# One decoder layer on one core: an expert's two column halves split over the contraction, or two experts side by side

## The chip, the cores and the metric

The kernel runs on 1 core of one Trainium2 chip. The metric is the device time of one execution in microseconds (us). Engines are named as in the profile: PE (TensorE, matrix products; its weight loads are listed as PEld), DVE (VectorE), ACT (ScalarE), POOL (GpSimd) and SP (SyncE, which issues the weight transfers).

## What is computed

One decoder layer over 512 tokens of width 1024: three attention branches, a gated merge with an output projection, a layer norm, then a mixture of 32 experts and a second norm. The change lies in the experts. Cut to that part, the reference is:

```
def hierarchical_moe(x, ...):
    # top-1 group of 4, then top-2 of the 8 experts in it; gate = p(group) * softmax(top-2 logits)
    ...
    def expert_block(args):
        xb, e = args
        h = jax.nn.silu(xb @ w_gate[e]) * (xb @ w_up[e])     # [1024, 512] each
        return h @ w_down[e]                                 # [512, 1024]
    ...
    y_assign = y_pad[dest] * gate_sorted[:, None]
    out = jax.ops.segment_sum(y_assign, tok_sorted, num_segments=N)
```

## The kernel before

**Stages.** Projections and attentions run first, then the output projection with the first norm and the routing, up to about 452 us of the profile. The rest is the experts, then the second norm. Everything the experts read is float32, and all 32 experts' weights are streamed: 32 x 6 pieces of 1 MB.

**Slots.** Each expert gets 64 slots, so a pair of experts (2p, 2p+1) fills 128 partitions. `Pair.select` (L720) makes a 0-1 matrix [token, slot]; `gather` (L729) multiplies it with the residual x1 (for p of 2 and more with `xb`, x1 as three bfloat16 parts made by `split3`, L798) to get the pair's inputs `xg`; `info` (L741) fetches the gates and token numbers `si`; `places` (L756) makes the opposite 0-1 matrix `sT`; `combine` (L779) multiplies `sT` with the pair's outputs `y_h` and `y_l` (high and low part) and DVE adds the result to x1 (L791).

**One expert.** `up` (L945) is one of the two products with a [1024, 512] matrix: 8 matmuls of 512 columns whose stationary operand is the 64 slots of one expert, so each uses 64 of the array's 128 columns. `colmm` (L938) sends the even contraction tiles to partitions 0 to 63 of a PSUM bank and the odd ones to 64 to 127; `fold` (L929) then adds the two halves with one ACT copy (L933) and one DVE add (L935). `hidden` (L953) is silu on ACT and the product with the gate on DVE, `turn` (L957) four transpositions and an ACT copy to `hT`, `down` (L971) the two halves (c = 0, 1) of the third product, each 4 matmuls, a fold, and a split into `y_h` and `y_l`.

**Order of the work.** PE runs the order in which the code is written (`manual_schedule`). The other engines' orders are chosen by a scheduler from the dependencies. `expert(e)` (L988) runs up (gate), the transpositions of the expert before, a part of the pair's gather or combine, up (up), then the third product of the expert before. PSUM has eight banks by tags: `gu` 2, `dn` 2, `cb` 2, `xgp` 1, `ht` 1; a gather uses `xgp`, `turn` and `info` use `ht`, and a combine of a token tile writes two banks, `cb` and `cb`, or `xgp` and `ht`.

**Weights.** A ring of 16 pieces (four pools) and five pieces in tiles that are free for a while (`xb`, `once`) hold the weights; SP issues the transfers in their order of use, each as soon as its ring tile is free. After expert 17 stands a loop over slots beyond an expert's 64 (L1139), which with these inputs runs no iteration. All engines meet at a barrier ahead of it. Ten pieces are requested ahead of the loop, and six ring tiles are given to its body.

**The end.** `last_expert` (L1047) and `last_sums` (L1065) finish the sums; the factors and offsets of the second norm are brought to all partitions by four matmuls with a row of ones (`spread`, L979).

Of the kernel before, what the change touches and what calls it, by code (L numbers as in the profile page):

```python
# [38 lines left out]
AHEAD = (10, 11, 2, 20, 21)  # L39
# [3 lines left out]
MID = 17  # L43
# [8 lines left out]
def layer(ctx, tc, xT, xn, memT, w_qk, w_v, w_mk, w_mv, w_g, w_o, rb, oh, ln, wr, br,  # L52
# [76 lines left out]
    # Projections run as jobs of a queue, each on one loaded weight tile, in pieces that fill  # L129
    # the tensor engine between the steps of the attentions.  # L130
# [39 lines left out]
    def proj_T(rhs_h, rhs_l, n, done):  # L170
        """128 columns of a projection, transposed: [column, token]"""
        def body(w):
            o = bank("pj")
            for k in range(0, KT, 2):
                mm3(o[:, :n], [(w[0][:, j * P:(j + 1) * P], w[1][:, j * P:(j + 1) * P], rhs_h[:, j, :], rhs_l[:, j, :])
                               for j in (k, k + 1)], start=k == 0, stop=k == KT - 2)
                yield 6 * max(n, 256) / 512 * 0.216
            done(o)
        return body

    def put_q(res):
        """per head of the pair: [hi; hi] and [lo; lo] of q / 8"""
# [13 lines left out]
    def put_k(res, n=S, dst=None):  # L196
        """per head of the pair: hi in its own half, lo in the other"""
# [10 lines left out]
    def add_v(name, first, v):  # L208
        """[token, head dims] of a branch's values, two token tiles at a time"""
# [26 lines left out]
    # softmax attention, one pair of heads and one tile of queries at a time  # L236
# [50 lines left out]
    def advance(unit, us):  # L287
        """one more unit of softmax attention enters; those inside go one step further"""
# [11 lines left out]
    # stick-breaking attention: weight = sigmoid(z_s) times the product of 1 - sigmoid(z_j) = sigmoid(-z_j)  # L300
    # over the keys j after s, up to the query
# [19 lines left out]
    # memory keys and values  # L321
# [46 lines left out]
    # 0 for keys before the query, else far below any score  # L368
# [82 lines left out]
    # 128 columns of the model width at a time: gates times branch outputs, then their part of the  # L451
    # output projection, added to the residual
# [75 lines left out]
    def fetch(e, j, c, t=None):  # L528
        """half of one of an expert's three weight matrices"""
# [11 lines left out]
    def prefetch(e, j, cs=(0, 1), ts=(None, None)):  # L541
        for c, t in zip(cs, ts):
            pieces[e, j, c] = fetch(e, j, c, t)
# [8 lines left out]
    for ct in range(6):  # L552
# [7 lines left out]
        if ct in (2, 4):  # L560
            lastw[0] = jobs.last
            prefetch(ct // 2 - 1, 0)
# [19 lines left out]
    def norm(t, sm, gb, sp):  # L582
        """layer norm of x1's tile t, whose sums lie in sm"""
# [25 lines left out]
    prefetch(1, 1, ts=(t[:, 0:HALF], t[:, HALF:2 * HALF]))  # L609
    prefetch(0, 2, ts=(t[:, 2 * HALF:], None))  # L610
    prefetch(1, 2)
    prefetch(2, 0)
    prefetch(2, 1, (0,))
# [31 lines left out]
    def route(t, xts):  # L645
# [8 lines left out]
        # the group with the largest logit, then the two largest experts in it  # L654
# [33 lines left out]
    def settle():  # L688
        """the weights of every token's two experts, and the tables of the slots"""
# [18 lines left out]
    class Pair:  # L708
        """the slots of experts 2p and 2p + 1: their tokens, gates, inputs and outputs"""
# [10 lines left out]
        def select(self, t, d=None):  # L720
            """who sits in the slots, as a 0-1 matrix [token, slot]"""
# [19 lines left out]
        def info(self):  # L741
# [10 lines left out]
            ve.tensor_copy(si[0:64, 3:4], sp[64:128, 1:2])  # L752
            self.gate = (si[0:64, 0:1], si[0:64, 3:4])
# [11 lines left out]
        def room(self, c, dt=F32R):  # L765
            """half the columns of y, as the sum of two parts if in F32R"""
# [31 lines left out]
    def split3(c):  # L798
        """half the columns of x1 as the sum of three bfloat16"""
# [23 lines left out]
    def project(t, cols=(0, 1)):  # L823
        """the rest of the output projection of a token tile, and its norm"""
# [84 lines left out]
        # (base + hi - 1) * 64 + (rank - 64 * hi), or a negative number for ranks below 64  # L909
# [5 lines left out]
    # experts  # L915
# [7 lines left out]
    prefetch(0, 1, ts=(t[:, 0:HALF], t[:, HALF:]))  # L923
    prefetch(2, 1, (1,))
    prefetch(3, 0)
    prefetch(3, 1)
    prefetch(2, 2, (0,))
    after(sc.preload_act_table(AF.Silu), last_act[0])
    def fold(dst, src, q=0):  # L929
        """the two column halves of a product, added, to dst if given"""  # L930
        a, b = H[q], H[1 - q]
# [21 lines left out]
    def hidden(g, u, gate):  # L953
        sc.activation(out=g, in_=g, func=AF.Silu)
        ve.scalar_tensor_tensor(out=u, in0=u, scalar=gate, in1=g, op0=ALU.mult, op1=ALU.mult)

    def turn(u):  # L957
        hp = bank3("ht")
        for k in range(4):
            pe.transpose(hp[:, k * 64:(k + 1) * 64], u[:, k * P:(k + 1) * P], ident[0:64, 0:64])  # L960
        hT = late[0].tile([P, 4, 64], F32, name="hT", tag="hT", bufs=2)
        sc.copy(hT.rearrange("p a b -> p (a b)"), hp[:, 0:256])
        return hT

    def product(e, hT, c):
        w = weights(e, 2, c)
        o = bank3("dn")
        colmm(o, 4, lambda k: hT[:, k, :], lambda k: w[:, k * 512:(k + 1) * 512])
        return o

    def down(e, hT, c):  # L971
        pair, q = pairs[e // 2], e % 2
        if q == 0:
            pair.room(c, F32 if e == NE - 2 and c == 1 else F32R)
        pair.finish(c, q, product(e, hT, c))
# [3 lines left out]
    def spread(t, c):  # L979
        """512 of the second norm's factors and offsets to every partition"""  # L980
        r = slice(c * 512, (c + 1) * 512)
        o = bank3("xgp")
        pe.matmul(o, ones[0], t[0][0:1, r], start=True, stop=True)  # L983
        sc.copy(t[1][:, r], o)

    held, lnb2, ones = [None], [], [None]

    def expert(e):  # L988
        """an expert's first two products; the third of the expert before it, and what its pair waits for"""
# [280 lines left out]
```

## Time and profile before

| what | value |
|---|---|
| time, three runs | 994.44 us median (994.25 to 994.84) |
| the profiled execution: its span, first to last instruction (its only own time on the page) | 995.3 us |
| PE busy / share of the span | 955.3 us / 96% |
| DVE busy | 585.9 us / 59% |
| ACT busy | 379.1 us / 38% |
| POOL busy | 31.4 us / 3% |
| bytes moved, mean rate | 248.64 MB, 250 GB/s |
| PE granted clock, mean | 0.986 |

A busy PE is the share of time in which a matmul record is open; records of neighbouring matmuls overlap, so how long a piece of work takes on PE is read from the start of its first record to the start of what follows. "x16" in a row counts merged records: one float32 matmul is two records.

### The profile page before, as it was taken

The page shows a single profiled execution, that of the slowest core. Times are in us where ns is not written, and L with a number is a line of the kernel's source. Part 1 is how long each engine was busy: PE and PEld are TensorE (multiplying, and loading weights), DVE is VectorE, ACT ScalarE, POOL GpSimd, SP SyncE. Part 2 cuts the span into 40 slices and gives each one's busy share as a digit, 9 for nine tenths or more (in the row PEclk, how much of TensorE's full clock was granted, in tenths as well). Part 3 has the DMA queues.
Part 4 walks back from the last instruction along what each step waited for, and adds up shares of the span by engine and source line. Part 5 has one row for each costly group of instructions (what it writes and reads, how often), then busy time and mean ns, then how long its engine had stood idle before and what let it go on. Part 6 is the DMA issues. An engine that isn't in the chain of part 4 may idle for free. (4 is left out here: it accounts for less than half of the span.)

```text
span 995.3 us, 14993 instructions
## 1 busy us (share of the span) xinstructions
PE 955.3 (96%) x5892; PEld 612.4 (62%) x5892; DVE 585.9 (59%) x1210; ACT 379.1 (38%) x707; POOL 31.4 (3%) x24
## 2 busy tenths in 40 slices
PE   6999999999999999999999999999979999999992
PEld 6888888776888888784644544545525445455331
DVE  5776777556655532787766455554454556544457
ACT  6465565546222223234623333323313333233333
POOL 2000000000000000410000000000000000000003
PEclk9999999999999999999999999999989999999996
DMA  8252332121644332688799999999938999997902
GB/s 298 64 157 72 101 107 76 52 85 44 239 151 157 118 104 87 231 358 351 274 359 376 408 394 393 391 397 403 390 148 312 415 421 420 420 419 301 411 2 85
DMA packets 43938, 248.64 MB, mean 250 GB/s; under 512 B 5682, under 2 KB 6873, under 8 KB 19417
## 3 DMA queue, kind: packets, MB, share of 16 engines
q1 hardware_dynamic: 42194, 246.80, 64.6%
q10 hardware_dynamic: 1672, 0.85, 0.4%
q8 instruction: 48, 0.79, 0.3%
q14 instruction: 24, 0.20, 0.1%
HBM read 245.53 MB, written 2.11 MB: 249 GB/s over the span
## 5 line engine op out<-in xcount | busy, mean ns | idle before, releaser
L940 PE MATMUL gu<-r,xg 128*64 128x512 f32 x992 | 228.8, 603 | 5.3 <-DVE sel L726 5.3
L940 PEld LDWEIGHTS gu<-r,xg 128*64 128x64 f32 x992 | 67.5, 138 | 130.5 <-issue 126.2
L104 DVE TENSOR_TENSOR wl<-wraw,wh 128x1024 fp32r<-128x1024 f32 (+2 forms) x71 | 81.0, 1146 | 85.8 <-ACT wh L103 85.6
L125 PE MATMUL pj<-xh,wh 128*128 128x512 f32 x304 | 120.6, 397 | 0.0
L126 PE MATMUL pj<-xh,wl 128*128 128x512 f32 x304 | 118.6, 390 | 1.1 <-DVE wl L104 1.1
L127 PE MATMUL pj<-xl,wh 128*128 128x512 f32 x304 | 118.7, 391 | 0.0
L940 PE MATMUL dn<-r,hT 128*64 128x512 f32 x504 | 114.8, 596 | 0.0
L933 ACT COPY lo<-gu 64x512 f32<-64x512 f32 x64 | 37.3, 583 | 189.4 <-PE gu L940 185.7
L103 ACT CAST wh<-wraw 128x1024 fp32r<-128x1024 f32 (+2 forms) x71 | 70.3, 990 | 77.5 <-PE z L127 23.5
L738 PEld LDWEIGHTS <-xb 128*128 128x128 bf16 x1344 | 75.1, 98 | 13.1 <-issue 12.2
L738 PE MATMUL xgp<-sel,xb 128*128 128x128 bf16 x1344 | 79.9, 219 | 0.0
L940 PEld LDWEIGHTS dn<-r,hT 128*64 128x64 f32 x504 | 34.4, 137 | 68.5 <-issue 66.3
L935 DVE TENSOR_TENSOR u<-gu,lo 64x512 f32<-64x512 f32 x32 | 21.7, 679 | 86.5 <-ACT lo L933 86.5
L125 PEld LDWEIGHTS pj<-xh,wh 128*128 128x128 f32 x304 | 57.0, 188 | 14.3 <-issue 2.1
L791 DVE TENSOR_TENSOR x<-x,cb 128x512 f32<-128x512 f32 x61 | 40.0, 675 | 43.7 <-PE cb L789 43.7
L126 PEld LDWEIGHTS pj<-xh,wl 128*128 128x128 f32 x304 | 57.1, 188 | 12.8 <-DVE wl L104 1.4
L127 PEld LDWEIGHTS pj<-xl,wh 128*128 128x128 f32 x304 | 57.1, 188 | 12.1
L933 ACT COPY lo<-dn 64x512 f32<-64x512 f32 x64 | 37.0, 577 | 67.8 <-PE dn L940 67.7
L104 DVE TENSOR_TENSOR y_l<-yo,y_h 64x512 fp32r<-64x512 f32 x62 | 42.5, 686 | 31.1 <-ACT y_h L103 29.9
L103 ACT CAST y_h<-yo 64x512 fp32r<-64x512 f32 x62 | 38.2, 617 | 50.5 <-DVE yo L935 50.4
L935 DVE TENSOR_TENSOR g<-gu,lo 64x512 f32<-64x512 f32 x32 | 21.8, 682 | 54.7 <-ACT lo L933 54.7
L935 DVE TENSOR_TENSOR yo<-dn,lo 64x512 f32<-64x512 f32 x62 | 42.7, 689 | 10.6 <-ACT lo L933 6.0
(622 smaller groups left out, 1444.8 us busy)
## 6 DMA issues: line engine op xcount, KB each, us to landing
r<-in_we_dram SPq DMA_DIRECT2D x186, 1024.0 KB, 8.5
wraw<-in_w_g_dram SPq DMA_DIRECT2D x32, 512.0 KB, 3.5
wraw<-in_w_qk_dram SPq DMA_DIRECT2D x14, 512.0 KB, 3.7
wraw<-in_w_v_dram SPq DMA_DIRECT2D x16, 384.0 KB, 3.3
wraw<-in_w_o_dram SPq DMA_DIRECT2D x8, 512.0 KB, 3.6
xb<-in_we_dram SPq DMA_DIRECT2D x3, 1024.0 KB, 7.0
xraw<-in_xT_dram SPq DMA_DIRECT2D x4, 512.0 KB, 6.2
x<-in_xn_dram SPq DMA_DIRECT2D x4, 512.0 KB, 5.8
```

Of the source, the lines that this page charges most:

```text
L103: sc.copy(dst_h, src)
L104: (gp if eng is gp else ve).tensor_tensor(out=dst_l, in0=src, in1=dst_h.bitcast(F32), op=ALU.subtract)
L125: pe.matmul(o, lh, rh, start=start and i == 0, stop=False)
L126: pe.matmul(o, ll, rh, start=False, stop=False)
L127: pe.matmul(o, lh, rl, start=False, stop=stop and i == n - 1)
L738: pe.matmul(o[:, j * P:(j + 1) * P], a, b, start=i == 0, stop=i == len(srcs) - 1)
L791: ve.tensor_tensor(out=x1[:, t, r], in0=x1[:, t, r], in1=o, op=ALU.add)
L933: sc.copy(lo[a], src[b])
L935: ve.tensor_tensor(out=dst[a], in0=src[a], in1=lo[a], op=ALU.add)
L940: pe.matmul(o[H[k % 2]], lhs(k), rhs(k), start=k < 2, stop=k >= n - 2)
```

## The change

Two experts of a pair now run side by side. `up(p, j)` and `down(p, hT, c)` alternate matmuls of expert 2p (to partitions 0 to 63) and of expert 2p+1 (64 to 127), each over its whole contraction, so a bank holds the finished product of both and nothing is folded (the loop over extra slots, which runs no iteration, keeps `colmm` and `fold`). Silu, gating, transposition and the split of the output are done once per pair on 128 partitions. `pair_step(p)` is: up (gate) of the pair; combine of token tiles 0 and 1 of the pair before; up (up); combine of tiles 2 and 3; the first half of the next pair's gather; the transpositions; the second half of the gather and `info`; the third product. The third product is no longer held back into the next expert.

The weights are requested by a list in the new order of use (`todo`, `ahead`), 14 pieces ahead of the loop instead of 10, and the loop's body shares two ring tiles. The factors of the second norm come by two broadcast transfers in place of `spread`. `turn` needs one `hT` of 128 columns instead of two of 64.

```diff
     def weights(e, j, c):
-        return pieces.pop((e, j, c)) if isinstance(e, int) and (e, j, c) in pieces else fetch(e, j, c)
+        if (e, j, c) not in pieces:
+            ahead(1)
+        return pieces.pop((e, j, c))
+
+    def pieces_of(p):
+        return [(e, j, c) for j in range(3) for c in range(2) for e in (2 * p, 2 * p + 1)]
+
+    todo = [x for p in range(16) for x in pieces_of(p)]
+    todo[4:15] = todo[4:6] + todo[8:15] + todo[6:8]
+    taken = [0]
+
+    def ahead(n, ts=()):
+        for i in range(n):
+            e, j, c = todo[taken[0]]
+            taken[0] += 1
+            pieces[e, j, c] = fetch(e, j, c, ts[i] if i < len(ts) else None)
...
-        def finish(self, c, q, o, inplace=False):
+        def finish(self, c, o):
             if self.y_h[c] is None:
-                fold(self.y_l[c], o, q)
+                sc.copy(self.y_l[c], o)
             else:
-                y = fold(None if inplace else ep.tile([P, 512], F32, name="yo", tag="g", bufs=1), o, q)
-                split(self.y_h[c][H[q]], self.y_l[c][H[q]], y[H[q]])
+                split(self.y_h[c], self.y_l[c], o)
...
-    def up(e, q, pair, j, t):
-        w = [weights(e, j, c) for c in range(2)]
+    def up(p, j):
         o = bank3("gu")
-        colmm(o, KT, lambda k: pair.xg[:, k, H[q]], lambda k: w[k // 4][:, k % 4 * 512:k % 4 * 512 + 512])
-        fold(t, o)
-        return t
+        for k in range(KT):
+            for q in range(2):
+                if k % 4 == 0:
+                    w = held[q] = weights(2 * p + q, j, k // 4)
+                pe.matmul(o[H[q]], pairs[p].xg[:, k, H[q]], held[q][:, k % 4 * 512:k % 4 * 512 + 512],
+                          start=k == 0, stop=k == KT - 1)
+        return o
...
+    def hidden(p, g, u):
+        gs = ep.tile([P, 512], F32, name="g", tag="g", bufs=1)
+        hs = ep.tile([P, 512], F32, name="u", tag="u", bufs=1)
+        sc.activation(out=gs, in_=g, func=AF.Silu)
+        ve.scalar_tensor_tensor(out=hs, in0=u, scalar=pairs[p].si[:, 0:1], in1=gs, op0=ALU.mult, op1=ALU.mult)
+        return hs
...
+    def down(p, hT, c):
+        pair = pairs[p]
+        pair.room(c, F32 if p == 15 and c == 1 else F32R)
         o = bank3("dn")
+        w = [weights(2 * p + q, 2, c) for q in range(2)]
+        for k in range(4):
+            for q in range(2):
+                pe.matmul(o[H[q]], hT[:, k, H[q]], w[q][:, k * 512:(k + 1) * 512], start=k == 0, stop=k == 3)
+        pair.finish(c, o)
...
+    def pair_step(p):
+        g = up(p, 0)
+        if p > 0:
             pairs[p - 1].combine((0,))
             pairs[p - 1].combine((1,), banks=("xgp", "ht"))
+        u = up(p, 1)
+        hs = hidden(p, g, u)
+        if p == 0:
             once.close()
             late[0] = ctx.enter_context(pool("late", side="right", waits="tile"))
             split_gates()
+        else:
+            pairs[p - 1].combine((2,))
+            pairs[p - 1].combine((3,), banks=("xgp", "ht"))
+        if p < 15:
+            pairs[p + 1].gather(0)
+        hT = turn(hs)
+        if p < 15:
+            pairs[p + 1].gather(1, "cb" if p == 0 else "xgp")
+            pairs[p + 1].info()
+        for c in range(2):
+            down(p, hT, c)
+        if p == 0:
             xb[0] = xbp.tile([P, 3, TT, D], BF16, name="xb", tag="xb")
             split3(0)
             split3(1)
             for t in range(TT):
                 sc.mul(x1[:, t, :], x1[:, t, :], ALPHA)
+        if p == 1:
             overflow_table()
+        if p != MIDP:
+            pairs[p].places()
+        if p == 15:
+            lnt = ring().rearrange("p (a b) -> p a b", b=D)
+            lnb2.append(lnt)
+            for i in range(2):
+                nc.sync.dma_start(lnt[:, i, :], ln[2 + i:3 + i, :].to_broadcast([P, D]))
...
-        experts(range(MID + 1))
-    for h in AHEAD:
-        prefetch(MID + h // 10, h % 10)
+        steps(range(MIDP + 1))
+    ahead(RA + RB + RC + RD - 2)
...
-        experts(range(MID + 1, NE - 1))
-        last_expert()
+        pairs[MIDP].places()
+        steps(range(MIDP + 1, 16))
```

How the instructions stand, at three places. First PE in the middle of the experts, before: the second half of a combine (L788, L789), then the third product (`dn`), which reads weights and `hT` alone.

```order
L788 MATMUL xgp<-y_h_4998,sT 128x512
L789 MATMUL xgp<-y_l_4999,sT 128x512
L788 MATMUL ht<-y_h_5013,sT 128x512
L789 MATMUL ht<-y_l_5014,sT 128x512
L940 MATMUL dn<-r_5303,hT 64x512 x4
L940 MATMUL dn<-r_5318,hT 64x512 x4
L940 MATMUL gu<-r_5342,xg 64x512 x4
L940 MATMUL gu<-r_5344,xg 64x512 x4
L960 MATMUL ht<-ident,u 128x64 x4
```

The same place of PE in the changed kernel: the same combine (now L796, L797), then at once the gather (L748) into the bank `xgp`.

```order
L796 MATMUL xgp<-y_h_5142,sT 128x512
L797 MATMUL xgp<-y_l_5143,sT 128x512
L796 MATMUL ht<-y_h_5159,sT 128x512
L797 MATMUL ht<-y_l_5160,sT 128x512
L748 LDWEIGHTS xb
L748 MATMUL xgp<-sel,xb 128x128
```

Between a combine that fills `xgp` and a gather that fills it again there stood a third product, an up product and transpositions; now nothing stands there. Second, VectorE around the same place, before: the adds of the combine (L791) with the fold (L935) and the gating (L955) between them.

```order
L791 TENSOR_TENSOR x_2546<-x_2546,cb 128x512
L935 TENSOR_TENSOR u<-gu,lo 64x512
L791 TENSOR_TENSOR x_2546<-x_2546,cb 128x512
L955 SCALAR_TENSOR_TENSOR u<-u,si,g 64x512
L791 TENSOR_TENSOR x_2546<-x_2546,xgp 128x512
L791 TENSOR_TENSOR x_2546<-x_2546,ht 128x512
```

VectorE there in the changed kernel: the gating (L967) of 128 partitions, then the four adds (L799), then `sT` (L770).

```order
L967 SCALAR_TENSOR_TENSOR u<-gu,si,g 128x512
L799 TENSOR_TENSOR x_2546<-x_2546,cb 128x512 x2
L799 TENSOR_TENSOR x_2546<-x_2546,xgp 128x512
L799 TENSOR_TENSOR x_2546<-x_2546,ht 128x512
L770 TENSOR_TENSOR sT<-si,cs 128x512
```

The add that empties `xgp` still stands behind the gating and two adds; one fold has gone. Third, VectorE at the end of the first pair, before: the last of `split3` (L805, L807; `r` is its remainder), the first pair's `sT` (L761), the selection of the third pair (L725, L726) and the next fold.

```order
L807 TENSOR_TENSOR xb<-r_4403,xb 128x512
L807 TENSOR_TENSOR xb<-r_4408,xb 128x512
L761 TENSOR_TENSOR sT<-si,cs 128x512
L725 TENSOR_SCALAR sel<-i128b,d_3752 128x128 x2
L726 SCALAR_TENSOR_TENSOR sel<-i128b,d_3752,sel 128x128 x2
L760 TENSOR_TENSOR si<-si,cs 128x4
L935 TENSOR_TENSOR g<-gu,lo 64x512
```

VectorE there in the changed kernel: the last of `split3` (L813, L815), `sT` (L770), which shares a tile with half of `split3`'s remainders, and at once the adds of the first combine.

```order
L813 TENSOR_TENSOR r_4361<-x_2546,xb 128x512
L815 TENSOR_TENSOR xb<-r_4356,xb 128x512
L770 TENSOR_TENSOR sT<-si,cs 128x512
L815 TENSOR_TENSOR xb<-r_4361,xb 128x512
L799 TENSOR_TENSOR x_2546<-x_2546,cb 128x512 x2
```

In both kernels `split3` can begin when the third product has read the piece that lies in `xb`. Before, the rest of the third products, the second pair's gather, three up products and the third pair's gather then stand on PE ahead of the first combine, which needs `sT`; now half of the third product and one up product of the pair (twice 16 records) stand there.

## Rows read from the trace of the kernel before

**Rows 1.** Windows: us, busy (instructions) by engine, clock, DMA share, GB/s.

```profile
560.40:592.40 32.00, 32.00 (x234) 15.80 (x230) 17.26 (x35) 10.16 (x19) 0.00 (x0) 1.00 1.00 392
824.00:856.00 32.00, 32.00 (x237) 15.82 (x233) 17.26 (x35) 10.16 (x19) 0.00 (x0) 1.00 1.01 420
```

**Rows 2.** Waits of PE from 452 us on: total us, times, longest.

```profile
PE ht L960 <- DVE u L955: 0.6, 1, 0.6
PE cb L788 <- ACT y_h L103: 0.3, 1, 0.3
PE cb L789 <- DVE y_l L104: 0.2, 1, 0.2
```

**Rows 3.** Timeline, PE, one pair: start us, us, line, operation, records.

```profile
560.42 3.65 PE L940 MATMUL gu<-r,xg 128*64 128x512 f32 x16
...
564.00 0.46 PE L960 MATMUL ht<-ident,u 64*128 64x64 f32 x4
...
564.39 0.50 PE L788 MATMUL cb<-y_h,sT 128*128 128x512 f32 x1
...
566.44 3.65 PE L940 MATMUL gu<-r,xg 128*64 128x512 f32 x16
...
570.02 0.50 PE L788 MATMUL cb<-y_h,sT 128*128 128x512 f32 x1
...
572.07 3.65 PE L940 MATMUL dn<-r,hT 128*64 128x512 f32 x16
...
575.56 3.60 PE L940 MATMUL gu<-r,xg 128*64 128x512 f32 x16
...
579.09 0.46 PE L960 MATMUL ht<-ident,u 64*128 64x64 f32 x4
...
579.48 2.85 PE L738 MATMUL xgp<-sel,xb 128*128 128x128 bf16 x48
...
582.27 3.65 PE L940 MATMUL gu<-r,xg 128*64 128x512 f32 x16
...
589.29 2.85 PE L738 MATMUL xgp<-sel,xb 128*128 128x128 bf16 x48
...
592.36 3.65 PE L940 MATMUL gu<-r,xg 128*64 128x512 f32 x16
```

**Rows 4.** Timeline, VectorE and ScalarE in the same pair.

```profile
572.59 0.74 DVE L955 SCALAR_TENSOR_TENSOR u<-u,si,g 64x512 f32<-64x512 f32 x1
573.25 0.67 DVE L791 TENSOR_TENSOR x<-x,xgp 128x512 f32<-128x512 f32 x1
573.85 0.68 DVE L791 TENSOR_TENSOR x<-x,ht 128x512 f32<-128x512 f32 x1
...
582.37 0.58 ACT L739 COPY xg<-xgp 128x512 f32<-128x512 f32 x1 [1.15 <-PE xgp L738]
```

**Rows 5.** Timeline, PE: eight float32 transpositions of 128 columns.

```profile
438.35 1.04 PE L640 MATMUL gu<-ident,x 128*128 128x128 f32 x8
```

**Rows 6.** Groups of PE by shape: the four matmuls of `spread`.

```profile
L983 PE MATMUL xgp<-r,ones 1*128 1x512 f32 x8 | 4.5, 640 | 0.0
```

**Rows 7.** Timeline around the loop that runs no iteration.

```profile
731.65 3.65 PE L940 MATMUL dn<-r,hT 128*64 128x512 f32 x16
...
737.77 0.68 DVE L104 TENSOR_TENSOR y_l<-yo,y_h 64x512 fp32r<-64x512 f32 x1 [0.68 <-ACT y_h L103]
...
740.59 6.53 PE L940 MATMUL gu<-r,xg 128*64 128x512 f32 x16 [5.29 <-DVE sel L726]
```

**Rows 8.** Groups of VectorE, 468 to 487 us: `split3`.

```profile
L805 DVE TENSOR_TENSOR r<-x,xb 128x512 f32<-128x512 f32 x8 | 5.4, 684 | 0.2 <-ACT xb L804 0.2
```

**Rows 9.** A wait of PE at 411 us, and windows behind two waits.

```profile
411.19 0.50 PE L125 MATMUL dn<-woh,mgh 128*128 128x512 f32 x1 [1.47 <-ACT mgh L103]
...
412.00:416.00 4.00, 4.00 (x11) 3.18 (x12) 2.06 (x12) 0.57 (x1) 0.00 (x0) 0.58 0.87 363
...
444.00:448.00 4.00, 3.30 (x36) 3.21 (x36) 3.42 (x27) 1.56 (x3) 0.00 (x0) 1.00 1.01 426
```

More of the change, by code (lines that the diff above doesn't have):

```diff
@@ L38 @@
 HALF = 2048
[L39 removed]
+MIDP = 8
 CW = 184
@@ L608, in layer @@
     t = xbp.tile([P, 3 * HALF], F32, name="xb", tag="xb")
[L609 to L613, printed above, removed]
+    ahead(3, [t[:, i * HALF:(i + 1) * HALF] for i in range(3)])
+    ahead(RA)
     i128 = cs[:, 0:128]
@@ L958, in turn @@
+    def turn(u, n=P):
         hp = bank3("ht")
         for k in range(4):
[L960 to L966 removed]
+            pe.transpose(hp[:, k * n:(k + 1) * n], u[:, k * P:(k + 1) * P], ident[0:n, 0:n])
+        hT = late[0].tile([P, 4, P], F32, name="hT", tag="hT", bufs=1)
+        sc.copy(hT[:, :, 0:n], hp[:, 0:4 * n].rearrange("p (k t) -> p k t", t=n))
+        return hT
@@ L986, in layer @@
-    held, lnb2, ones = [None], [], [None]
-    def expert(e):
-        p, q = divmod(e, 2)
-        prev = held[0]
-        g = up(e, q, pairs[p], 0, row("g"))
-        if prev is not None:
-            hT = turn(prev)
-        if e == NE - 2:
-            lnt = (ring(), ring())
-            nc.sync.dma_start(lnt[0][0:1, :], ln[2:4, :].rearrange("(o a) b -> o (a b)", o=1))
-            lnb2.append(lnt[1].rearrange("p (a b) -> p a b", b=D))
-            ones[0] = late[0].tile([1, P], F32, name="ones", tag="ov", bufs=1)
-            ve.memset(ones[0], 1.0)
-            spread(lnt, 0)
-        if q == 0 and 0 < p < 15:
-            pairs[p + 1].gather(0)
-        elif q == 1 and p > 0:
+        w = [weights(2 * p + q, 2, c) for q in range(2)]
@@ L1005, in expert @@
+        for k in range(4):
+            for q in range(2):
+                pe.matmul(o[H[q]], hT[:, k, H[q]], w[q][:, k * 512:(k + 1) * 512], start=k == 0, stop=k == 3)
+        pair.finish(c, o)
+    sm2 = rpool.tile([P, TT, 8], F32, name="sm2")
+    held, lnb2 = [None, None], []
+    def pair_step(p):
+        g = up(p, 0)
+        if p > 0:
             pairs[p - 1].combine((0,))
             pairs[p - 1].combine((1,), banks=("xgp", "ht"))
-        u = up(e, q, pairs[p], 1, row("u"))
-        hidden(g, u, pairs[p].gate[q])
@@ L1009, in expert @@
-        held[0] = u
-        if e == NE - 2:
-            spread(lnt, 1)
-        for c in range(2):
-            if q == 1 and p > 0 and c == 0:
-                pairs[p - 1].combine((2,))
-                pairs[p - 1].combine((3,), banks=("xgp", "ht"))
-            if prev is not None:
-                if e == 1 and c == 1:
-                    hT1 = turn(u)
-                down(e - 1, hT, c)
-                if e == NE - 2:
-                    spread(lnt, 2 + c)
-        if q == 0 and p > 0:
-            pairs[p - 1].places()
@@ L1024, in expert @@
-        if e == 1:
-            for c in range(2):
-                down(1, hT1, c)
-            held[0] = None
-            pairs[1].gather(0)
-            pairs[1].gather(1, "cb")
-            pairs[1].info()
-        elif q == 0 and 0 < p < 15:
-            pairs[p + 1].gather(1)
-            pairs[p + 1].info()
-        if e == 0:
+        u = up(p, 1)
+        hs = hidden(p, g, u)
+        if p == 0:
             once.close()
@@ L1043, in expert @@
                 sc.mul(x1[:, t, :], x1[:, t, :], ALPHA)
-        if e == 3:
+        if p == 1:
             overflow_table()
-    def last_expert():
-        e = NE - 1
-        g = up(e, 1, pairs[15], 0, row("g"))
-        hT = turn(held[0])
-        pairs[14].combine((0,))
-        pairs[14].combine((1,), banks=("xgp", "ht"))
-        u = up(e, 1, pairs[15], 1, row("u"))
-        hidden(g, u, pairs[15].gate[1])
-        pairs[14].combine((2,))
-        pairs[14].combine((3,), banks=("xgp", "cb"))
-        down(e - 1, hT, 0)
-        hT1 = turn(u)
-        down(e - 1, hT, 1)
-        hT = hT1
-        pairs[15].places()
-        down(e, hT, 0)
-        down(e, hT, 1)
+        if p != MIDP:
[5 more added lines that the diff above has]
+                nc.sync.dma_start(lnt[:, i, :], ln[2 + i:3 + i, :].to_broadcast([P, D]))
     def last_sums(c):
@@ L1122, in choose, with steps @@
             pairs[p].select(t)
-    def experts(es):
-        for e in es:
-            if e % 2 == 0 and e // 2 + 1 < 16:
-                choose(e // 2 + 1)
-            expert(e)
+    def steps(ps):
+        for p in ps:
+            if p + 1 < 16:
+                choose(p + 1)
+            pair_step(p)
     with tc.manual_schedule(engines={mybir.EngineType.PE}):
         pairs[0].info()
-        experts(range(MID + 1))
-    for h in AHEAD:
-        prefetch(MID + h // 10, h % 10)
+        steps(range(MIDP + 1))
+    ahead(RA + RB + RC + RD - 2)
     ovi, dv = over
```

58 lines of the change are left out of this document (22 added, 36 removed).

## Prediction

> **What bounds the kernel now.** I first read the windows of single pairs: from 560 to 592 us PE is busy for the whole of 32.00 us at clock 1.00, VectorE for 17.26 and ScalarE for 10.16 [rows 1]. Then the list of waits: in the whole expert stage PE waits for other engines in four places, three of them small [rows 2], the fourth the loop that runs no iteration, 5.29 us [rows 7]. So the experts are a chain of PE work without gaps, and what counts is how long each piece takes from start to start [rows 3]: one pair from 560.42 to 592.36, that is 31.94 us. Weight transfers are close behind: their engines are busy throughout at 392 GB/s, the rate at which PE frees ring tiles; later they reach 420 [rows 1], at which the pair's 12.58 MB take 30.0 us. Transfers therefore bind only if a pair falls under 30.0 us. The folds that the change removes lie on engines that nobody waits for. Removing them gives nothing by itself; the gain must come from PE's own records, and the loss from what PE newly waits for.
>
> **The products themselves.** Before, even and odd contraction tiles already run side by side in the two halves of the columns; now two experts do. Matmuls, columns and pairing stay 8 per up product and expert, 4 per half of a third product: 0.
>
> **Fewer interruptions.** An up product alone takes 560.42 to 564.00, 3.58 us; two in a row take 572.07 to 579.09, 7.02 us [rows 3]. So each separate run of half-array matmuls costs 2 x 3.58 - 7.02 = 0.14. Before, I count 68 runs (3 in the first pair, 4 in each of the next 14, 8 in the last, one cut by the loop); now 33 (third product and next up product together, the other up product alone). 35 x 0.14 = **-4.9 us**. Bounds: 0, if the cost goes with the other kind of work, and the full -4.9.
>
> **Transpositions.** 32 sets of four of 64 columns, 564.00 to 564.39: 0.39 each [rows 3], 12.5 in all. Now 16 sets of four of 128 columns; eight take 1.04 [rows 5], four 0.52: 8.3. **-4.2**.
>
> **The norm's factors.** Four `spread` matmuls are open for 4.5 us on PE [rows 6]; less a little overlap **-4.3**. The broadcast transfers that replace them follow the last weights in SP's queue, into a tile that the pair's third product before last frees, some 35 us ahead of their use: 0.
>
> **The first pair** loses PE's wait for the gating, 0.6 [rows 2]: **-0.6**.
>
> **The loop.** All engines meet ahead of it. PE's last record ends at 731.65 + 3.65 = 735.30, VectorE's at 738.45, 3.15 later, behind two folds and splits; PE goes on 2.14 after that [rows 7]. Now a ScalarE pass of 0.6 and a VectorE pass of 0.68 follow PE's last record [rows 4, 7], about 1.4 in all: **-1.7**. The clock: the next product takes 6.53 instead of 3.65 [rows 7]; the idle time stays 3.5 us, so I leave that as it is (bounds 0 and -2.9).
>
> **A new wait at `xgp`, each pair.** There is one such bank. A combine's last tile fills it, and the gather that wants it next now stands right behind. Take the end of the up product as 0, when the gating can start: the combine holds PE for 570.02 to 572.07 = 2.05 [rows 3]. VectorE starts the gating at about 0.1, then the adds: gating to add 0.66, add to add 0.60, the `xgp` add itself 0.67 [rows 4]. It ends at 0.1 + 0.66 + 2 x 0.60 + 0.67 = 2.65 to 2.75, and PE follows some 0.05 later: a wait of 0.65 to 0.75, **0.70**. Before, the same add ended at 573.92, 1.85 after the combine, under a third product that does not use the bank. The second half of the gather waits for the ScalarE copy of the first: that copy starts 0.10 after the next work on PE and takes 0.58 (gather at 579.48, next work 582.27, copy 582.37) [rows 3, 4]; transpositions cover 0.52 of 0.73, the bf16 gather's shorter end leaves some more: **0.3** (bounds 0.2 and 0.4). Both hit pairs 1 to 14: 14 x 1.0 = **+14.0**. What is queued behind them on PE is the whole rest of the pair, so nothing hides them. If VectorE were quicker, or the bank free, the bound is 0.
>
> **The first combine.** It needs the first `sT`, which stands behind 17 VectorE passes (15 of `split3`, two splits). These start when the first half of the third product ends and ScalarE has made the first cast, about 0.7 later; a pass is 0.68 long and the next starts 0.60 to 0.66 on [rows 4, 8]: 18 x 0.64 + 0.7 = 12.2, and some 1.5 for casts that VectorE waits for, since both engines alternate on two remainder tiles: 13.7. PE has 3.5 + 7.0 = 10.5 us of products until then. Wait **+3.3** (bounds 1.5 and 5). Behind a wait of 1.47 the granted clock was 0.58 over the next 4 us, so part of them at half, 1.2 for 2.4 GHz: 0.42 x 4 = 1.7 us lost; where idle time left 3.30 of 4.00 us busy it stayed at 1.00 [rows 9]. Behind the loop's 5.29 the loss was 2.9, 6.53 for 3.65 [rows 7]. I take **+1.7** here (bounds 0 and 2.9).
>
> **The end.** The last pair has no gather to put between combine and transpositions. Those use the bank `ht`, whose add ends 0.6 after that of `xgp`: wait 1.3. Then `hT` is copied before the third product can start: 0.1 + 0.58 + 0.05, 0.8 in all. Before, waits of 0.5 stood here [rows 2]: **+1.6**; and half a chance of 1.7 for the clock: **+0.8**.
>
> **Sum.** -4.9 - 4.2 - 4.3 - 0.6 - 1.7 = -15.7; +14.0 + 3.3 + 1.7 + 1.6 + 0.8 = +21.4; net **+5.7 us**. A pair takes 31.94 - 0.28 (two runs fewer) - 0.26 (transpositions) + 1.0 = 32.4. The profiled execution's span, 995.3, stands 0.9 above the median of the runs; the differences are of its rows, so I add them to the median: 994.4 + 5.7 = **1000.1 us**.
>
> **The rivals.** (1) *The bank waits are not there.* VectorE's add may be done when the gather wants `xgp`. For: VectorE is idle for nearly half of a pair [rows 1]. Against: its order has the gating ahead of the adds, and the sum above has no slack in it. It gives 1000.1 - 14 = 986 us, faster. The point from which it decides is the wait of a pair, both halves: under 0.6 us the kernel is no slower, under 0.45 it is faster by more than 0.2%. (2) *The waits are partly hidden*, a pair losing 0.5 to 0.75, and the first combine waits less: 993 to 996.4, no change that a measurement here can tell (0.2%, 2 us, is the least). (3) *The clock falls in every pair*: two waits and the transpositions lie within 5 us, 14 x 1.7 = +24, 1024 us. Against it, the window from 444 to 448 has the same share of idle time, 0.70 of 4 us, and clock 1.00 [rows 9]. The Trainium skill, "TensorE: Matmul & The Clock Gate", Part 4, says that transposes do not count as PE activity for the gate in the way matmuls do, which would make this rival likelier than the idle time alone does; by that rule the time is the 1024 just given. No trace here has such transpositions between two waits. (4) *Transfers bind*: under 30.0 us a pair, which no case reaches; the deeper request ahead of the loop, 14 for 10, only helps.
>
> **Chances.** The forecast with its own range, 996.4 to 1005 (unknown costs: bank waits 0.85 to 1.2 a pair, first combine 1.5 to 5, clock 0 to 2.9 in three places): 0.68. Rival 1: 0.10, below 992.4. Rival 2: 0.16, of which 0.03 ends below 992.4. Rival 3: 0.06. The range leaves out most of rival 1 and rival 3: 991 to 1005. Faster 0.13, same 0.14, slower 0.73.
>
> **What would show it.** In the list of waits: the gather at L748 waiting for VectorE's adds (L799), 14 times about 0.7, and for ScalarE's copy (L749), 14 times about 0.3; one wait of about 3 at the first combine (L796), with a half clock behind it; at the end waits of about 1.3 and 0.8 at L973 and L985; a pair of 32.4 us from up product to up product; the loop's gap at 3.5. The folds gone from VectorE and ScalarE without effect on PE. The forecast is wrong if those waits at L748 are missing or half as long, if a pair takes under 32 us, or if the clock falls inside every pair.

## The result and the profile after

The changed kernel took 1001.51 us (median of 11 runs, 998.06 to 1003.66); the kernel before, timed beside it, 996.05 (11 runs). The ratio is 1.0057, 95% interval 1.0044 to 1.007: slower by 5.5 us by the medians and by 5.7 by the ratio, where 5.7 was predicted. The difference is small, but the interval lies clear of 1. In the profiled executions the stretch from the first up product to the end went from 995.3 - 452.33 = 543.0 to 999.7 - 451.37 = 548.3 us, +5.4, so the two traces can be compared piece by piece.

Busy times of the changed kernel, from its page: VectorE and ScalarE lost 116 and 108 us of work (585.9 and 379.1 before), PE 12.9 (955.3 before), and none of it shows in the time.

```profile
PE 942.4 (94%) x5820; PEld 613.3 (61%) x5820; DVE 469.9 (47%) x1034; ACT 271.3 (27%) x513; POOL 30.6 (3%) x24
```

The list of PE's waits over the expert stage (total us, times, longest) answers to [rows 2] and the last line of [rows 7]:

```profile
PE xgp L748 <- DVE x L799: 9.7, 14, 0.7
PE gu L958 <- DVE sel L735: 6.9, 1, 6.9
PE xgp L748 <- ACT xg L749: 3.2, 14, 0.2
PE cb L796 <- ACT xb L814: 2.7, 1, 2.7
PE ht L973 <- DVE x L799: 1.3, 1, 1.3
PE dn L985 <- ACT hT L975: 0.7, 1, 0.7
```

Before, PE's waits were worth 1.1 us and the loop's 5.29; these six lines hold 24.5. Five of them are waits that the prediction named, with its counts; the second, the loop, is the one it got wrong. (The fourth is put down to ScalarE, but `sT` on VectorE ran from 489.67 to 490.36, and PE started at 490.51.)

PE's timeline of one pair answers to [rows 3]:

```profile
556.83 0.50 PE L796 MATMUL cb<-y_h,sT 128*128 128x512 f32 x1
...
565.88 0.50 PE L796 MATMUL cb<-y_h,sT 128*128 128x512 f32 x1
...
567.60 0.39 PE L797 MATMUL ht<-y_l,sT 128*128 128x512 f32 x1
568.69 2.84 PE L748 MATMUL xgp<-sel,xb 128*128 128x128 bf16 x48 [0.70 <-DVE x L799]
571.37 0.61 PE L973 MATMUL ht<-ident,u 128*128 128x128 f32 x4
572.20 2.84 PE L748 MATMUL xgp<-sel,xb 128*128 128x128 bf16 x48 [0.23 <-ACT xg L749]
...
575.25 7.09 PE L985 MATMUL dn<-r,hT 128*64 128x512 f32 x32
582.17 7.04 PE L958 MATMUL gu<-r,xg 128*64 128x512 f32 x32
589.13 0.50 PE L796 MATMUL cb<-y_h,sT 128*128 128x512 f32 x1
```

A pair lasts from 556.83 to 589.13, 32.30 us (31.94 before, 32.4 predicted). VectorE's timeline beside it answers to [rows 4]: the gating, two adds, and the add that empties `xgp`, which ends at 568.63, 0.06 ahead of the gather.

```profile
566.10 0.75 DVE L967 SCALAR_TENSOR_TENSOR u<-gu,si,g 128x512 f32<-128x512 f32 x1 [6.01 <-PE gu L958]
566.76 1.28 DVE L799 TENSOR_TENSOR x<-x,cb 128x512 f32<-128x512 f32 x2
567.95 0.68 DVE L799 TENSOR_TENSOR x<-x,xgp 128x512 f32<-128x512 f32 x1
```

The clock, in windows as in [rows 9]: behind the first combine's wait at 490.51, inside a pair with both its waits (568 to 576), and behind the loop.

```profile
488.00:492.00 4.00, 1.49 (x4) 1.23 (x5) 3.20 (x6) 3.82 (x6) 0.00 (x0) 0.75 1.01 426
492.00:496.00 4.00, 4.00 (x16) 1.99 (x16) 2.40 (x4) 0.00 (x0) 0.00 (x0) 0.82 1.02 424
...
568.00:572.00 4.00, 3.28 (x52) 3.11 (x52) 1.84 (x4) 0.43 (x1) 0.00 (x0) 1.00 1.02 424
572.00:576.00 4.00, 3.80 (x64) 3.37 (x65) 0.60 (x5) 1.24 (x3) 0.00 (x0) 1.00 1.00 412
...
752.00:756.00 4.00, 4.00 (x12) 0.97 (x10) 1.14 (x6) 0.00 (x0) 0.00 (x0) 0.50 0.95 397
```

The chain that ended last, cut to the loop (start, us, what), has no answer among the rows of before:

```profile
736.89 3.63 PE dn L985 x16
740.53 0.30 SPq L533
...
740.92 7.22 DMA r<-in_we_dram
...
749.04 0.69 DVE sT L770
...
750.81 4.53 PE gu L958 x9
```

The first half of the last third product ahead of the loop ends and frees two ring tiles; SP requests pieces 13 and 14 of the 14; the landing of the last, 7.22 us later, opens the barrier.

### The profile page after: what moved, and what is told of

Read it like the earlier page. It is cut to its first block, busy times and chain, and to the rows that moved or that the text cites. A ratio compares the mean times of both kernels' runs of the same rounds, so it can differ in the third digit from the quotient of the medians.

```text
span 999.7 us, 14330 instructions
## 1 busy us (share of the span) xinstructions
PE 942.4 (94%) x5820; PEld 613.3 (61%) x5820; DVE 469.9 (47%) x1034; ACT 271.3 (27%) x513; POOL 30.6 (3%) x24
## 4 chain that ended last, share of the span: by engine, by line
PE 83%; DVE 9%; ACT 3%; issue 3%; DMA 1%; SPq 0%; DVEq 0%; POOL 0%; ACTq 0%; POOLq 0%
PE gu L958 20%; PE dn L985 11%; PE pj L124 9%; PE pj L126 8%; PE xgp L748 8%; PE pj L125 8%; DVE x L799 3%; PE z L126 2%; PE z L125 2%; PE z L124 2%; PE y L278 2%; PE z L267 1%; DVE u L967 1%; PE cb L796 1%; ACT xg L749 1%
## 5 line engine op out<-in xcount | busy, mean ns | idle before, releaser
L958 PE MATMUL gu<-r,xg 128*64 128x512 f32 x992 | 221.7, 600 | 6.9 <-DVE sel L735 6.9
L958 PEld LDWEIGHTS gu<-r,xg 128*64 128x64 f32 x992 | 70.3, 138 | 146.6 <-issue 146.2
L748 PE MATMUL xgp<-sel,xb 128*128 128x128 bf16 x1344 | 79.5, 219 | 12.9 <-DVE x L799 9.7
L748 PEld LDWEIGHTS <-xb 128*128 128x128 bf16 x1344 | 77.3, 98 | 20.0 <-issue 20.0
L749 ACT COPY xg<-xgp 128x512 f32<-128x512 f32 x29 | 17.0, 585 | 240.8 <-PE xgp L748 240.8
L799 DVE TENSOR_TENSOR x<-x,cb 128x512 f32<-128x512 f32 x60 | 38.5, 681 | 84.0 <-PE cb L797 84.0
L967 DVE SCALAR_TENSOR_TENSOR u<-gu,si,g 128x512 f32<-128x512 f32 x16 | 12.0, 751 | 102.1 <-PE gu L958 84.1
L103 DVE TENSOR_TENSOR y_l<-dn,y_h 128x512 fp32r<-128x512 f32 x31 | 21.4, 691 | 74.3 <-ACT y_h L102 74.3
L102 ACT CAST y_h<-dn 128x512 fp32r<-128x512 f32 x31 | 18.1, 585 | 90.0 <-PE dn L985 90.0
L761 DVE COPY si<-ht 128x3 f32<-128x3 f32 x16 | 2.6, 160 | 82.5 <-PE ht L758 78.6
L385 ACT ACTIVATE gt<-pj 128x512 f32<-128x512 f32 x24 | 14.3, 598 | 89.9 <-PE pj L126 89.9
L966 ACT ACTIVATE g<-gu 128x512 f32<-128x512 f32 x16 | 9.5, 597 | 105.5 <-PE gu L958 105.5
```

Of the source, the lines that this page charges most:

```text
L102: sc.copy(dst_h, src)
L103: (gp if eng is gp else ve).tensor_tensor(out=dst_l, in0=src, in1=dst_h.bitcast(F32), op=ALU.subtract)
L748: pe.matmul(o[:, j * P:(j + 1) * P], a, b, start=i == 0, stop=i == len(srcs) - 1)
L749: sc.copy(self.xg[:, 4 * c:4 * c + 4, :], o.rearrange("p (k t) -> p k t", t=P))
L799: ve.tensor_tensor(out=x1[:, t, r], in0=x1[:, t, r], in1=o, op=ALU.add)
L958: pe.matmul(o[H[q]], pairs[p].xg[:, k, H[q]], held[q][:, k % 4 * 512:k % 4 * 512 + 512], start=k == 0, stop=k == KT - 1)
```

## Experiments

Theory: what PE gains in products, transpositions and `spread` is eaten by waits that stand on PE's chain, one bank above all. Rivals: the waits only mark time that would be lost elsewhere (transfers, the clock), or the new order of products is slow in itself.

**1. Another bank for the gather.**

```
-            pairs[p + 1].gather(0)
+            pairs[p + 1].gather(0, "dn" if p else "xgp")
```

> The first half of each gather goes to the bank pair `dn`, which is free then, instead of `xgp`; nothing else changes. Theory (the bank holds PE, 0.70 + 0.23 a pair): both waits at L748 vanish from the list, a pair falls from 32.30 to 31.37 us, and the time by 14 x 0.93 = 13.0: 7.3 us less than the kernel before. Rival (the work behind it waits in its place, for `ht`, for `hT` or for `dn`): waits of the same sum under other names, pair 32.3, no change to the changed kernel, 5.7 more than before. Rival (transfers bind): a pair stays above 31.9 with waits for the DMA at L958 or L985.

Measured: 985.88 us, ratio 0.9906 (0.9891 to 0.9921): 15 us below the changed kernel, 2 more than expected; its profiled span, 983.6, is 16.1 below, though its end lost 1.7 to the clock. Its list of waits has no L748 left. PE's timeline of a pair:

```profile
829.52 7.09 PE L985 MATMUL dn<-r,hT 128*64 128x512 f32 x32
...
854.18 0.39 PE L797 MATMUL ht<-y_l,sT 128*128 128x512 f32 x1
854.41 2.85 PE L748 MATMUL dn<-sel,xb 128*128 128x128 bf16 x48
857.10 0.61 PE L973 MATMUL ht<-ident,u 128*128 128x128 f32 x4
857.54 2.84 PE L748 MATMUL xgp<-sel,xb 128*128 128x128 bf16 x48
...
860.61 1.94 PE L985 MATMUL dn<-r,hT 128*64 128x512 f32 x8
```

A pair takes 860.61 - 829.52 = 31.09, 1.2 less, though the waits were listed at 0.93. From the last combine matmul to the gather it is 0.23 here and was 1.09 (567.60 to 568.69): the wait of 0.70 cost 0.86. From the transpositions to the second half it is 0.44 and was 0.83: 0.39 for 0.23. The 0.16 more is the overlap of two records, which a wait takes away. The Trainium skill, "TensorE: Matmul & The Clock Gate", Part 2, says that the next matmul starts while the last one drains and that a lone one can't hide that; the 0.16 fits this. The rivals fall: nothing waits in place of the bank, and no transfer.

**2. The gating put last in the code.** `hidden` was called behind the combine instead of ahead of it.

> VectorE's gating pass is put behind the combine's adds; bank and PE's order stay. Theory (the add that empties `xgp` is late because one pass of 0.66 stands ahead of it): the wait for VectorE at L748 falls from 0.70 to about 0.04 in 14 pairs, that for ScalarE stays 0.2; 14 x 0.66 = 9.2 us less than the changed kernel, 3.5 less than before. The gated values are then ready 3.4 us after the up product and needed at 4.8, so the transpositions don't wait. Rival (the wait is the bank's turn from PE's writing to the next writing and not VectorE's order): 0.5 to 0.7 stays, no change. Rival (the gating becomes the wait): 0.3 or more a pair at L973.

Measured: 1001.75 us, ratio 1.0068 (1.0054 to 1.0082), with the changed kernel's list of waits. This tests nothing: the scheduler kept the gating in its old place, and VectorE's order was the same as in the changed kernel. It is a second measurement of the changed kernel, and as such it shows one thing. The wait at the first combine is there again, but PE runs at full clock behind it:

```profile
489.65 0.47 PE L796 MATMUL cb<-y_h,sT 128*128 128x512 f32 x1 [2.74 <-ACT xb L814]
...
491.64 7.09 PE L958 MATMUL gu<-r,xg 128*64 128x512 f32 x32
```

The combine takes 491.64 - 489.65 = 1.99 us, 3.37 in the changed kernel's profile (490.51 to 493.88). Of the nine traces that have this wait, the half clock stands behind it in four (the changed kernel, experiments 1, 3 and 10) and not in five (2, 5, 6, 8 and 9). Experiment 6 forces the order.

**3. Fewer pieces ahead of the loop.**

```
-    ahead(RA + RB + RC + RD - 2)
+    ahead(12)
```

> Ahead of the loop 12 pieces are requested instead of 14. Theory (the barrier waits until the last requested pieces have landed; two of them are requested only when PE frees their tiles at 740.4 us, and land near 749): the loop's gap on PE falls from 6.9 to about 3.5, the time by 3.4, 2.3 us above the kernel before; the transfers left out come later and nobody waits for them. Rival (the gap is VectorE's last split and the barrier itself): gap 6.9, no change. Rival (the pieces left out are missed behind the loop): the gap falls but waits for the DMA of 2 to 5 us come after it.

Measured: 998.62 us, ratio 1.0034 (1.0021 to 1.0048), 2.3 us below the changed kernel. PE's first product behind the loop:

```profile
748.49 9.11 PE L958 MATMUL gu<-r,xg 128*64 128x512 f32 x32 [4.95 <-DVE sel L735]
```

The gap falls by 1.95, not by 3.4: the landing held the barrier, but not alone. VectorE's last split ends at 744.89, 1.35 behind PE's last product, which is the 1.4 that the prediction had. VectorE's first pass behind the barrier starts 1.42 later (1.43 before), but PE's first product 2.18 after that; before it was 0.71. That 1.5 us is not explained. Yet PE's own gap of 4.95 is about that of the two traces of the old order (5.29 before, 5.01 in experiment 7), though VectorE's last pass ends 3.15 behind PE's last record there and 1.35 here.

**4. The first `sT` ahead of `split3`.**

```
-            d = late[0].tile([P, 512], F32, name="r3", tag=("sT", "sq")[t % 2], bufs=1)
+            d = ep.tile([P, 512], F32, name="r3", tag=("g", "u")[t % 2], bufs=1)
...
+            pairs[0].places()
             xb[0] = xbp.tile([P, 3, TT, D], BF16, name="xb", tag="xb")
...
-        if p != MIDP:
+        if p not in (0, MIDP):
             pairs[p].places()
```

> The first pair's `sT` is made ahead of the 15 passes of `split3`, whose remainders use other tiles. Theory: the wait of 2.7 at the first combine and the half clock behind it (1.3) vanish, 4.0 us less than the changed kernel, 1.7 more than before. Rival (the combine then waits for the splits of the first pair's result, or VectorE's adds come late behind `split3` and hold the next combine): 1 to 2.7 of the wait comes back at L796 or L748, and the change is under 2 us.

Measured: 998.69 us, ratio 1.0031 (1.0019 to 1.0042), about 2.6 below the changed kernel. PE's timeline there, without a wait or a half clock:

```profile
480.89 7.04 PE L958 MATMUL gu<-r,xg 128*64 128x512 f32 x32
487.85 0.50 PE L796 MATMUL cb<-y_h,sT 128*128 128x512 f32 x1
...
489.90 7.09 PE L958 MATMUL gu<-r,xg 128*64 128x512 f32 x32
```

From the up product to the next: 9.01 us, 13.14 in the changed kernel (480.74 to 493.88), 4.1 for the 4.0 expected. That is against an execution whose clock fell there; against experiment 2, where it did not (479.87 to 491.64, 11.77), it is 2.8. The runs gained 2.6, nearer to the second. The shift of the trace lasts to the last pair. There this execution lost 1.6 again: the third products behind the waits of 1.26 and 0.73 took 8.6 us at a clock of 0.57, where the changed kernel's profile has 7.0 at 1.00. So it went in four of seven traces that have these two waits.

**5. The last pair's transpositions between the two combines.**

```
             pairs[p - 1].combine((2,))
+            if p == 15:
+                hT = turn(hs, bank="gu")
             pairs[p - 1].combine((3,), banks=("xgp", "ht"))
...
```

(In the other pairs `turn` stays where it was.)

> In the last pair alone the transpositions stand between the two combines of the pair before, in the bank `gu`. Theory: the waits of 1.26 at L973 and 0.73 at L985 vanish, and with them the half clock that followed them in three of five traces (the last third products took 8.7 us there, 7.0 elsewhere): 2.0 to 3.9 us less than the changed kernel, 1.8 to 3.7 more than before; in its trace the last 32 records of L985 take 7.0 at clock 1.00. Rival (the copy of `hT` or the gating takes their place): one wait of 0.5 to 1 at L985 stays and the gain is under 1.5.

Measured: 998.78 us, ratio 1.0038 (1.0025 to 1.0052), about 2 below the changed kernel. Both waits are gone from the list, and the third products take 970.05 - 963.03 = 7.02:

```profile
963.03 7.09 PE L985 MATMUL dn<-r,hT 128*64 128x512 f32 x32
970.05 0.50 PE L796 MATMUL cb<-y_h,sT 128*128 128x512 f32 x1
```

They took 7.02 in the changed kernel's profile too, so this trace shows the waits gone, and not a gain from the clock. The runs gained about the 2.0 of the waits, the least that was expected.

**6. The adds ahead of the gating**, with an order between the two passes that the scheduler keeps (one profiled execution).

> As the kernel with the gating put last, but now VectorE's four adds do stand ahead of the gating pass (in that kernel the order on VectorE had stayed as it was). By the prediction's chain, which begins with the gating, the wait at L748 falls from 0.70 by 0.66 to 0.04 and the pair to 31.45 us. By the later reading, in which the first add can't begin before PE has filled the first `cb` (0.77 after the combine's start, as in the first half of a combine, where no gating stands ahead), it falls by 0.10 to 0.60, the pair to 32.2, the time by 1.4.

Measured: 998.58 us (995.14 beside it). From PE's list of waits, and VectorE's first add behind the up product:

```profile
PE xgp L748 <- DVE x L799: 8.4, 14, 0.6
```

```profile
565.31 1.29 DVE L799 TENSOR_TENSOR x<-x,cb 128x512 f32<-128x512 f32 x2 [6.58 <-PE cb L797]
```

0.60, as the later reading has it. The add starts 0.77 after the combine (564.54) without a gating pass ahead and 0.88 after it with one (566.76 - 565.88): all but 0.1 of the gating lies beside PE's first two combine matmuls. The prediction had the length of the wait right and its first link wrong.

**7. The old kernel without `spread`.** The broadcast transfers alone, in the kernel before.

```
...
-            spread(lnt, 0)
+            for i in range(2):
+                nc.sync.dma_start(lnb2[0][:, i, :], ln[2 + i:3 + i, :].to_broadcast([P, D]))
```

(The other three `spread` calls are gone too, with the row of ones and the transfer that they read.)

> The kernel before with one part of the change alone: the factors of the second norm come by two broadcast transfers, and the four `spread` matmuls are gone. Theory: PE loses four stretches of 1.05 us on a chain without gaps, 4.2 us less than the kernel before (ratio 0.9958). Rival (the broadcast holds the weights behind it in SP's queue): a wait of PE for a DMA in the last two pairs, and a gain under 2. Rival (the four did not stand on the path): no change.

Measured: 990.20 us, ratio 0.995 (0.9937 to 0.9963): 5.0 less. On PE the stretch from the product ahead of the four to the transpositions behind them:

```profile
932.82 3.60 PE L940 MATMUL gu<-r,xg 128*64 128x512 f32 x16
...
947.20 0.46 PE L960 MATMUL ht<-ident,u 64*128 64x64 f32 x4
```

14.38 us, where the kernel before took 19.03: 4.65 less, 4.2 for the four and 0.45 for the runs that they cut.

**8. The banks of the second two token tiles exchanged.**

```
-            pairs[p - 1].combine((2,))
-            pairs[p - 1].combine((3,), banks=("xgp", "ht"))
+            pairs[p - 1].combine((2,), banks=("xgp", "ht"))
+            pairs[p - 1].combine((3,))
```

> The changed kernel with the banks of the second two token tiles exchanged: token tile 2 goes to `xgp` and `ht`, token tile 3 to `cb` twice. Theory (the bank is held because its add is the third of a chain of four passes of 0.6 that begins when PE has filled the first bank): the add of `xgp` is now the first and ends before PE reaches the gather; the waits of 0.70 vanish in 14 pairs, and that of 1.26 for `ht` in the last; each gives back 0.16 more, the overlap of two records. 14 x 0.86 + 1.4 = 13.4 us less than the changed kernel, 7.7 less than before. The wait of 0.23 for ScalarE stays. Rival (what counts is VectorE's load between combine and gather, not the order in it): 0.5 or more of the wait stays.

Measured: 987.86 us, ratio 0.9926 (0.9914 to 0.9939): 13 us below the changed kernel. Same passes, same banks, another order. In its list of PE's waits those for VectorE's adds, at L748 and L973, are gone. At the bank the wait for ScalarE's copy is left, as expected:

```profile
PE xgp L748 <- ACT xg L749: 3.2, 14, 0.2
```

**9. One run of half-array matmuls cut in two** (one profiled execution; against experiment 1).

```
             pairs[p + 1].gather(1, "cb" if p == 0 else "xgp")
-            pairs[p + 1].info()
+            if p == 0:
+                pairs[p + 1].info()
         for c in range(2):
             down(p, hT, c)
+            if 0 < p < 15 and c == 0:
+                pairs[p + 1].info()
```

> The changed kernel with half of the gather in `dn`, and in pairs 1 to 14 the 12 small matmuls of `info` stand between the two halves of the third product instead of ahead of it. Nothing is added, but one run of half-array matmuls is cut in two. Theory (each cut costs 0.14, as the term for fewer interruptions has it): the pair is 31.08 + 0.14 = 31.22 us, the whole 2.0 longer than with the gather alone moved. Rival (the cost went with the kind of work, not with the cuts): 31.08. Only the period of the pairs in its trace tells this apart.

Measured: 986.82 us (995.14 beside it). PE's timeline:

```profile
825.32 2.85 PE L748 MATMUL dn<-sel,xb 128*128 128x128 bf16 x48
...
831.23 3.65 PE L985 MATMUL dn<-r,hT 128*64 128x512 f32 x16
834.82 0.46 PE L758 MATMUL ht<-gmb,sel 128*128 128x3 bf16 x12
835.21 3.65 PE L985 MATMUL dn<-r,hT 128*64 128x512 f32 x16
838.69 7.04 PE L958 MATMUL gu<-r,xg 128*64 128x512 f32 x32
...
856.66 2.85 PE L748 MATMUL dn<-sel,xb 128*128 128x128 bf16 x48
```

The pair is 856.66 - 825.32 = 31.34, 0.25 more. The cut third product takes 3.59 + 3.48 = 7.07 for 6.91 (829.52 to 836.43 in experiment 1): 0.16, the term's 0.14. The other 0.09 lies where the gather now meets a half-array product instead of `info`.

**10. A longer wait at the bank.** Two useless passes ahead of the add that empties `xgp` (one profiled execution).

```
             pairs[p - 1].combine((2,))
-            pairs[p - 1].combine((3,), banks=("xgp", "ht"))
+            if p < 15:
+                junk = late[0].tile([P, 512], F32, name="junk", tag="sq", bufs=1)
+                for i in range(2):
+                    more = ve.tensor_tensor(out=junk, in0=x1[:, 2, 512:1024], in1=x1[:, 2, 0:512], op=ALU.add)
+            pairs[p - 1].combine((3,), banks=("xgp", "ht"), behind=more if p < 15 else None)
```

> Two more VectorE passes without use stand ahead of the add that empties `xgp`, and `sT` with them, so that add ends some 2.1 us later in each of 14 pairs. The wait at L748 is then about 2.8 instead of 0.70. Theory (a wait of this length, alone in a pair, costs the clock as the one of 2.73 at the first combine does): half clock behind each, 14 x (2.1 + 1.3) = 48 us, 1049 in all. Rival (the clock stays as it does at 0.70 and 0.23): 14 x 2.1 = 29 us, 1031, and 1.00 in the windows behind the waits. If the VectorE passes have less effect than that, the wait says so.

Measured: 1037.28 us (995.14 beside it), some 36 above the changed kernel and between the two. From PE's list of waits, and its timeline in two pairs:

```profile
PE xgp L748 <- DVE x L799: 36.8, 14, 2.7
```

```profile
574.23 4.08 PE L748 MATMUL xgp<-sel,xb 128*128 128x128 bf16 x48 [2.71 <-DVE x L799]
578.10 1.04 PE L975 MATMUL ht<-ident,u 128*128 128x128 f32 x4
...
645.70 2.84 PE L748 MATMUL xgp<-sel,xb 128*128 128x128 bf16 x48 [2.71 <-DVE x L799]
```

The waits alone give 36.8 - 9.7 = 27.1. The clock falls behind some of them, and not behind each: the gather took 3.9 to 4.3 us instead of 2.67 in 5 of the 14 pairs, all among the 12 with a wait of 2.71.

**11. Experiments 1, 3, 4 and 5 together.**

> The four changes together: half of the gather in `dn`, 12 pieces ahead of the loop, the first `sT` ahead of `split3`, and the last transpositions between the combines. Theory (the costs stand one behind the other on PE, so they add up): 15.6 + 2.4 + 4.0 + 2.0 to 3.9 less than the changed kernel, that is 975 to 978 us, 18 to 20 less than before. Rival (with the waits gone the weights don't come in time): PE waits for a DMA at L958 or L985, and 2 to 6 us of it are lost.

Measured: 976.11 us, ratio 0.9809 (0.9797 to 0.9822): 19 us faster than before. One wait is left on PE, the loop's, and the transfers run at the rate of [rows 1] (the row's last number):

```profile
PE gu L958 <- DVE sel L735: 5.0, 1, 5.0
```

```profile
856.00:888.00 32.00, 32.00 (x232) 16.09 (x230) 8.31 (x16) 3.44 (x6) 0.00 (x0) 1.00 1.02 421
```

The time lies within the range given. Measured one by one the four changes gave 15.0, 2.3, 2.6 and 1.9, 21.8 us by their ratios, and together 24.7. The 3 us more are not explained; the mean clock that was granted, 0.983 to 0.985 in the runs of experiment 1 and 0.988 to 0.990 here, may be part of it. So the change itself, without the waits that its order brought, is the faster kernel.

## Why the prediction held, step by step

**The bank, +14.0.** Shown. 14 waits of 0.70 and 14 of 0.23: moving half of the gather to another bank (experiment 1) takes both away, and the order of two banks alone (8) those of 0.70. Its working had two errors that offset each other in the pair's 32.4: a wait costs 0.16 more than it is listed with (1.25 a pair, 17.5 in all), and a pair without waits takes 31.09, not 31.4. And the gating, counted with 0.66, adds only 0.10 to the wait (6); the chain begins when PE has filled the first `cb`.

**Fewer runs and transpositions, -4.9 and -4.2.** Right, and somewhat small. A pair's four products took 2 x 3.58 + 2 x 7.02 = 21.20 [rows 3]; now 13.88 (575.25 to 589.13) + 7.02 (558.86 to 565.88) = 20.90, so -0.30 for -0.28; a cut by itself costs 0.16 (9). Transpositions 0.44 for 2 x 0.39, -0.34 for -0.26. The rest of the 0.85, some 0.2, lies in combines, gathers and `info`, which now follow each other; no experiment takes it apart.

**`spread`, -4.3.** -5.0 alone in the old kernel (7), 4.65 in its trace.

**The loop, -1.7.** This step failed, in its sign. The gap went from 5.29 to 6.90, the clock's part from 2.9 to 2.7 (9.69 for 7.02), +1.4 in all. The working took it for granted that what VectorE does last opens the barrier and that PE goes on a fixed time after it, and rival 4 even said that the deeper request "only helps". With 14 of 16 tiles requested, the last requests wait for the last third product, and the barrier for their landing, as the chain above shows. Taking two requests away gave back 1.95 (3). Nor does the gap follow VectorE where no landing holds it: VectorE's last pass ended 3.15 behind PE's last record in the two traces of the old order and 1.35 behind in experiments 3 and 11, and the gap was 5.29 and 5.01 there, 4.95 and 5.04 here. So the shorter work on VectorE, from which the -1.7 was taken, gave PE next to nothing. What sets the 5 us is open.

**The first combine, +3.3 and +1.7.** The wait is right, 2.73. The clock is right for the profiled execution, 1.3 (493.88 - 490.51 = 3.37 for 2.05), but that was luck: it was entered in full, and it came in four of the nine traces with this wait (2). Its price was taken from the wait of 1.47 at 411 us [rows 9]; a wait of 1.31 to 1.68 stands there in all 13 traces, and the clock fell behind it in three (the kernel before, experiments 4 and 9). Both costs go when `sT` is made earlier (4).

**The end, +1.6 and +0.8.** The waits are right: 1.26 and 0.73, less the 0.5 of before. The clock falls in four of the seven traces with these waits, for 1.6 us, and not in the changed kernel's profiled execution. The half chance was a fair price; which execution it hits is not explained.

**The folds.** They were worth nothing, as said: 224 us of work less on two engines, for which PE had waited 1.1 us in all outside the loop.

**The rivals.** (1) and (2) fall with the waits, which are there in full. (3): no clock fell inside a pair of the changed kernel, 1.00 in the windows around both waits and the transpositions. The rule of the Trainium skill ("TensorE: Matmul & The Clock Gate", Part 4) on transposes is not borne out as a cost here: experiment 1 has the same transpositions without a wait at 1.00 too. (4): no pair waited for a transfer, at 31.09 us neither.

So the sum of +5.7 came out as measured because errors cancel: the loop was 3.1 us too low; the first combine 1.0, the 14 pairs 1.4 (0.36 each for 0.46), the end 0.9 (0.8 of it for a clock that did not fall) and `spread` 0.4 too high, by the profiled execution. The mechanism that was priced highest, the bank, is the one that decides the sign; that the sum met the measurement within 0.3 us is luck.

## What to carry to other kernels

When work is moved, list for each PSUM bank who filled it last and who must empty it before the next writer, and count from the first matmul of the filling group; the order of banks in a group of four was worth 13 us here. Price a wait of PE with what its neighbours no longer overlap as well, and a half clock behind it with a chance. Ahead of a barrier, ask not only which engine comes last but which transfer lands last, and when it could be requested at all.

## What was not expected of the hardware

The same wait does not always cost the clock. Behind 12 waits of 2.71 in one execution PE ran at half clock for part of the next gather five times and at full clock seven times; behind the 2.73 of the first combine it did so in four of nine executions, for 1.3 to 1.5 us; behind waits of 1.26 and 0.73 close together it did so in four of seven executions, for 1.6 us. Behind 0.70 and 0.23 in a pair it never did. A clock loss read from one profile is therefore a chance and not a cost, until other executions show it.

Behind the barrier of the loop PE restarted 0.41 and 0.71 us after VectorE in the two traces of the old order and 1.20 to 2.26 after it in the eleven of the new order. The profile puts PE's wait down to `sel`, which that product does not read; no run here tells what it waits for.
